# Hyena filter product on one core: second matmul over 128 partitions in place of 64

## Chip, cores and metric

The kernel runs on one core of a Trainium2 chip. The metric is the device time of one execution in microseconds. Three runs of the kernel before took 2377.81, 2381.3 and 2377.95 us, with a median of 2377.95 us.

## What is computed

The reference is a two-layer network over 256 latent and 256 context tokens of width 1024. Each layer is a half-step SwiGLU, a token mixing of two branches (gated linear attention, and an order-2 Hyena convolution), and a second half-step SwiGLU. The part that the change touches makes the Hyena filters, once for each layer, from positions alone:

```python
def hyena_filters(L, f_w1, f_b1, f_fr1, f_w2, f_b2, f_fr2, f_w3):
    ...
    h = jnp.sin(f_fr1 * (z @ f_w1 + f_b1))
    h = jnp.sin(f_fr2 * (h @ f_w2 + f_b2))
    h = (h @ f_w3).astype(jnp.float32).reshape(L, 2, HY_ORDER, HY_WIDTH)
    ...
    return h * window[:, None, None, :]
```

Here L is 256, the hidden width 64, and `f_w3` has 4096 columns (2 directions, 2 orders, 1024 channels). The product `h @ f_w3` is the one in question.

## The kernel before, in words

Activations lie with features on the partitions and 512 tokens (context, then latent) along the free axis. Weights come as chunks of eight 128x128 tiles (512 KB). Each chunk is loaded by SP, cast on ScalarE to a high part `whi` (L221), and VectorE subtracts to get the low part `wlo` (L222); up to three split chunks are kept. Every product of the layers is then three matmuls of the fp32r type (`mm3`, L382 to L384): high times high, high weight times low activation, low weight times high activation. In the stages `ffn1h` (gate and up) and `ffn1d` (down) of layer 0 and of layer 1, where both streams are worked on, those matmuls have 512 columns.

Beside these projections a second kind of work is laid into the program by `Fill`: generators that advance some steps after each projection (`fill.slot()`), in two lanes, at a pace set by deadlines counted in projections. Two of them run beside `ffn1`: `ada_gen` (modulation vectors, on VectorE at L639, fed by its own loads `adat`) and `filter_gen`, which makes the Hyena filters. The order of all instructions on an engine is thus fixed when the program is built.

`filter_gen` first makes the hidden activation `h2` (L879 to L882). Its weights `fw2` are stored twice side by side, so rows 64 to 127 of `h2` repeat rows 0 to 63. `h2s[:, 0]` is the high part and `h2s[:, 1]` the low part, each 128 rows by 256 positions. The third weights are stored twice one above the other; `split_w3` (L899) leaves their high part in rows 0 to 63 of `w3` and their low part in rows 64 to 127. Then, for each of 4 channel quarters and 2 orders, one step multiplies them. It takes two banks of PSUM (tile names ending in `_x_fil`), and for two halves of the positions (`par`) and two directions (`d`) it issues a pair of matmuls: the first (L922) has all 128 rows, high part of `h2` against high and low weights at once; the second (L923) has the low part of `h2` against the high weights and uses rows 0 to 63 alone. The position half of `h2s` is the stationary operand (128 columns), and `w3` streams 256 columns past it. So a step is eight matmuls, and there are eight steps in each layer, 16 in the program. VectorE then multiplies both banks by a window (L925, L926), and later steps normalise the filters (L939 to L954) and transform them with `mm3` on the tiles `_x_fdft` (L956 to L960).

Of the kernel before, what the change touches and what calls it, by code (L numbers as in the profile page):

```python
# [46 lines left out]
HY_HIDDEN = 64  # L47
# [27 lines left out]
def first_units():  # L75
    """The first hidden tiles of the whole program, in the order of their rows."""
    out = []
    for k in range(KT):
        for j in range(FIRST):
            out += mat("ffn1_w_gate", 0, j * P, [k])  # L80
            out += mat("ffn1_w_up", 0, j * P, [k])
    return out
# [119 lines left out]
class WS:  # L202
    """The stream of weight tiles: loaded in the order of use, split into a high and a low part."""
# [21 lines left out]
    def need(self, tiles):  # L225
        """Loads what the next tiles take."""
        for i in range((self.pos + tiles - 1) // CHUNK + 1):
            self._load(i)

    def ahead(self, tiles, i):  # L230
        """Loads the i-th chunk of those that start the given number of tiles from here, out of turn and into a pool that
        has room."""
        pos = self.pos + tiles
        while pos < len(self.plan) and self.plan[pos] is None:
            pos += 1
        self._load(pos // CHUNK + i, True)
# [40 lines left out]
class Fill:  # L277
    """Work that runs in the shadow of the projections, a few steps after each of them, at the pace that its deadline
    (counted in projections) asks for. In every step the tensor engine's part comes first and rests only on earlier
    steps."""  # L280
# [40 lines left out]
def build(tc, a, dbg=None):  # L321
    nc = tc.nc
    with ExitStack() as ctx:
# [27 lines left out]
        def opnd(w, p=actp, tag="act", name="op"):  # L351
            """High and low part of a matmul operand, w columns each."""
            if w == T:
                t = pair(p=p, tag=tag, name=name)
                return t[:, 0], t[:, 1]
            if spare.get(name):
                return spare.pop(name)
            t = pair(p=p, tag=tag, name=name)
            spare[name] = (t[:, 1, :L], t[:, 1, L:])
            return t[:, 0, :L], t[:, 0, L:]  # L360

        def plain(n, w, name):
            """n fp32 tiles of w columns."""
            out = []
            while len(out) < n:
                t = pair(F32, name=name).rearrange("p a b -> p (a b)")
                out += [t[:, i * w:(i + 1) * w] for i in range(2 * T // w)]
            return out
# [10 lines left out]
        mm = nc.tensor.matmul  # L379
# [48 lines left out]
        def quad_sum(srcs, kind, between=lambda: None):  # L428
            """Sums over the partitions of each tile: row 32 j + any of the result holds tiles j, j + 4, ... added up."""
            n = srcs[0].shape[-1]  # L430
            st = bank(kind)
            rounds = len(srcs) // 4
            for r in range(rounds):
                if r:
                    between()
                for j in range(4):
                    mm(st[32 * j:32 * j + 32, :n], lhsT=ones[:, :32], rhs=srcs[r * 4 + j], start=r == 0, stop=r == rounds - 1)
            ss = t2((P, n), name="ss")
            nc.scalar.copy(ss, st[:, :n])
            return ss  # L440

        def inv_sqrt(out, src):
            """(src) ** -0.5 for a few columns in SBUF."""
            nc.gpsimd.tensor_tensor(out=out, in0=src, in1=half[:, :src.shape[-1]], op=ALU.pow)

        def rstd(ms):
            """1 / rms of tokens, from their mean squares and epsilon."""
            nt = ms.shape[-1]
            r = sm.tile([P, nt], F32, tag="rs", name=nm("rs"))
            inv_sqrt(r, ms)  # L450
            return r

        def spread(r):
            """The same along the free axis of all partitions."""
            pr = bank("nbc")
            for i in range(r.shape[-1]):
                mm(pr[:, i * P:(i + 1) * P], lhsT=r[:, i:i + 1].broadcast_to([P, P]), rhs=ident, start=True, stop=True)
            return pr[:, :r.shape[-1] * P]
# [6 lines left out]
        class Squares:  # L465
            """Mean squares of the tokens, as the feature tiles are done: all but the last two for both streams at once."""
# [48 lines left out]
        def norm_gen(l, m, s, h, sums):  # L515
            """The norm of one stream, in steps between which the tensor engine does other things."""
            sh, sca = mods[(l, m)], mods[(l, m + 1)]
            vv = 1 - s
            r = rstd(sums.total(s))
            yield  # L520
            r = spread(r)
            if sums.early is not None:
                sums.early.r = t2((P, L), name="r")
                nc.scalar.copy(sums.early.r, r)
            for k in range(KT):
                modulate(k, s, r, sca[:, vv, k:k + 1], sh[:, vv, k:k + 1], h)
                if k % 2:
                    yield

        class Early:  # L530
            """Products of the latent tokens before their norm is known: with x * scale, and with the shift in a column of its
            own. The norm's factor comes in afterwards."""
# [32 lines left out]
        class Beside:  # L565
            """Runs the steps of a generator at given counts of calls."""
# [14 lines left out]
        def v_part(o, wv, h, tt, k):  # L581
            """Values of a tile of tokens, token-major."""
            xh, xl = h[k][0][:, tt * P:(tt + 1) * P], h[k][1][:, tt * P:(tt + 1) * P]
            mm(o, lhsT=xh, rhs=wv[k][0], start=k == 0, stop=False)
            mm(o, lhsT=xh, rhs=wv[k][1], start=False, stop=False)
            mm(o, lhsT=xl, rhs=wv[k][0], start=False, stop=k == KT - 1)

        def first_split(jobs, h, pend, v=None):
            """The first products after a norm, stream by stream: jobs are (result by stream, weights). Besides, values of
            the first stream's tokens."""  # L590
# [18 lines left out]
        def mod_finish(l, m, raw, nv):  # L609
            """raw[:, v, j]: j-th feature tile of modulation m for vector v (0 latent, 1 context)."""  # L610
# [11 lines left out]
        def ada_gen(ms):  # L622
            # silu(c) along the free axis
# [27 lines left out]
        def start():  # L651
            """First norm and first hidden tiles, a feature tile at a time as its modulation arrives. The tensor engine's
            clock is kept up while it waits for the first data."""
# [132 lines left out]
        def out_tiles(take, src, gate, streams, after):  # L786
            """The products of src that go into x, and the next norm unless x is not done yet."""
# [32 lines left out]
        def tail(take, src, gate, sums, after):  # L820
            """The last two output tiles, one stream after the other, so that the next norm of the first runs beside
            the second. Returns the norm of the second, to be run."""
# [43 lines left out]
        def filter_gen(l):  # L866
# [32 lines left out]
            def split_w3(wb):  # L899
                """High part above, low part below."""  # L900
# [12 lines left out]
            for q in range(NQ):  # L913
                for o in range(2):
# [3 lines left out]
                    for par in range(2):  # L918
                        cp = slice(par * P, (par + 1) * P)
                        for d in range(2):  # L920
                            f = pf[d][:, par * CQ:(par + 1) * CQ]
                            mm(f, lhsT=h2s[:, 0, cp], rhs=w3[:, d], start=True, stop=False)  # L922
                            mm(f, lhsT=h2s[:HY_HIDDEN, 1, cp], rhs=w3[:HY_HIDDEN, d], start=False, stop=True)  # L923
# [61 lines left out]
        def la_gen(l, asp, wap, bs):  # L985
            """Cumulative log decays (times 16) within the chunks, for every head and direction."""
# [94 lines left out]
        def gla_core(l, hd, bs, kT, qT, vp, rp, og):  # L1081
# [23 lines left out]
            def attend(d):  # L1105
                """Masked scores within tiles of two chunks. From the tile's first chunk (in the order of the scan) to its
                second, keys decay to the end of the one and queries from the start of the other."""
# [10 lines left out]
            def widen(d):  # L1118
                """From chunks to tiles: keys decay to the end of the tile, queries from its start."""
# [17 lines left out]
            def update(d):  # L1137
                """The state at the start of every tile."""
# [72 lines left out]
        def short_conv(l, j, ps, c, both):  # L1211
            """c[:, t] = w0 u[t-1] + w1 u[t] + w2 u[t+1] + b along rows (context: one row, latent: grid rows)."""
# [15 lines left out]
        def hy_proj(l, q, h):  # L1228
            """Returns z (time-major, [t, stream, channel] for the even and for the odd time steps, split), x1 (likewise, as
            it is) and x2 (channel-major)."""  # L1230
# [129 lines left out]
        def hy_conv_lat(l, q, z, x1, x2, z3):  # L1360
            """The same for the latent tokens alone: real and imaginary parts, or even and odd time steps, side by side."""
# [211 lines left out]
def fold(x):  # L1573
    """(rows, cols) with rows = k * 128 + p  ->  (128, k * cols)"""
    r, c = x.shape
    return x.reshape(r // P, P, c).transpose(1, 0, 2).reshape(P, (r // P) * c)
# [88 lines left out]
```

## Time and profile before

| what | value |
|---|---|
| median of 3 runs | 2377.95 us |
| runs | 2377.81, 2377.95, 2381.3 us |
| span of the profiled execution, first to last instruction | 2375.0 us |
| median run less that span | 2.95 us |
| TensorE busy, of the span | 2358.3 us |
| VectorE busy | 1666.0 us |
| ScalarE busy | 946.9 us |
| mean granted TensorE clock | 0.998 |

The profiled execution has no time of its own beside its span, so the span is set against the median run. PE is TensorE's matmuls, PEld its weight loads, DVE VectorE, ACT ScalarE, POOL GpSimd. A matmul's duration in the trace reaches into that of the next, because they are pipelined; what a stream of them costs is read from start to start. Its entry names the rows used of the array, as in 64\*128, and the operand that streams, as in 64x256.

### The profile page before, as it was taken

The page shows a single profiled execution, that of the slowest core. Times are in us where ns is not written, and L with a number is a line of the kernel's source. Part 1 is how long each engine was busy: PE and PEld are TensorE (multiplying, and loading weights), DVE is VectorE, ACT ScalarE, POOL GpSimd, SP SyncE. Part 2 cuts the span into 40 slices and gives each one's busy share as a digit, 9 for nine tenths or more (in the row PEclk, how much of TensorE's full clock was granted, in tenths as well). Part 3 has the DMA queues.
Part 4 walks back from the last instruction along what each step waited for, and adds up shares of the span by engine and source line. Part 5 has one row for each costly group of instructions (what it writes and reads, how often), then busy time and mean ns, then how long its engine had stood idle before and what let it go on. Part 6 is the DMA issues. An engine that isn't in the chain of part 4 may idle for free.

```text
span 2375.0 us, 33612 instructions
## 1 busy us (share of the span) xinstructions
PE 2358.3 (99%) x13300; PEld 2039.0 (86%) x13300; DVE 1666.0 (70%) x2613; ACT 946.9 (40%) x1422; POOL 114.4 (5%) x102
## 2 busy tenths in 40 slices
PE   9999999999999999999999999999999999999998
PEld 6788888888888888898888898888888999999998
DVE  4876775666779989677577756656566888868554
ACT  4432333544433334432222333323334555646444
POOL 0000011000000000010000010000011000001001
PEclk9999999999999999999999999999999999999999
DMA  7544444232243333436556535445343233555553
GB/s 273 188 146 148 156 152 151 92 107 98 98 133 124 124 116 101 140 109 201 177 169 205 176 119 166 148 146 163 125 140 116 73 128 126 168 180 173 185 186 125
DMA packets 108126, 347.52 MB, mean 146 GB/s; under 512 B 12014, under 2 KB 19008, under 8 KB 107968
## 3 DMA queue, kind: packets, MB, share of 16 engines
q1 hardware_dynamic: 107968, 345.37, 44.4%
q8 instruction: 104, 1.70, 0.3%
q14 instruction: 54, 0.44, 0.1%
HBM read 332.74 MB, written 12.58 MB: 145 GB/s over the span
## 4 chain that ended last, share of the span: by engine, by line
PE 92%; DVE 4%; issue 1%; ACT 1%; DMA 1%; POOL 1%; POOLq 0%; DVEq 0%; SPq 0%; ACTq 0%
PE L1ffn1h_acc_main L382 3%; PE L1ffn1h_acc_main L383 3%; PE L0ffn2h_acc_main L382 3%; PE L1ffn1h_acc_main L384 3%; PE L0ffn2h_acc_main L383 3%; PE L0ffn2h_acc_main L384 3%; PE L0ffn1h_acc_main L382 3%; PE L0ffn1h_acc_main L384 3%; PE L0ffn1h_acc_main L383 3%; PE L0hy_acc_main L384 2%; PE L0hy_acc_main L382 2%; PE L0hy_acc_main L383 2%; PE L1ffn2h_acc_main L382 2%; PE L1ffn2h_acc_main L383 2%; PE L1ffn2h_acc_main L384 2%; PE L0ffn1d_acc_main L382 2%
## 5 line engine op out<-in xcount | busy, mean ns | idle before, releaser
L221 ACT CAST whi<-raw 128x1024 fp32r<-128x1024 f32 x440 | 460.7, 1049 | 844.1 <-issue 311.4
L222 DVE TENSOR_TENSOR wlo<-raw,whi 128x1024 fp32r<-128x1024 f32 x440 | 538.2, 1225 | 213.3 <-ACT whi L221 210.9
L639 DVE SCALAR_TENSOR_TENSOR trash<-adat,sc 128x1024 bf16<-128x1024 f32 x224 | 275.8, 1231 | 170.6 <-DMA adat<-in_adaT 166.9
L382 PE MATMUL L1ffn1h_acc_main<-h,whi 128*128 128x512 f32 (+1 forms) x376 | 144.2, 384 | 0.0
L384 PE MATMUL L1ffn1h_acc_main<-h,wlo 128*128 128x512 f32 (+1 forms) x376 | 142.1, 378 | 0.0
L383 PE MATMUL L1ffn1h_acc_main<-h,whi 128*128 128x512 f32 (+1 forms) x376 | 142.0, 378 | 0.0
L384 PE MATMUL L0ffn2h_acc_main<-h,wlo 128*128 128x512 f32 (+1 forms) x376 | 141.2, 376 | 0.0
L383 PE MATMUL L0ffn2h_acc_main<-h,whi 128*128 128x512 f32 (+1 forms) x376 | 141.2, 376 | 0.0
L382 PE MATMUL L0ffn2h_acc_main<-h,whi 128*128 128x512 f32 (+1 forms) x376 | 141.0, 376 | 0.0
L382 PE MATMUL L0ffn1h_acc_main<-h,whi 128*128 128x512 f32 x304 | 120.4, 396 | 0.0
L384 PE MATMUL L0ffn1h_acc_main<-h,wlo 128*128 128x512 f32 x304 | 118.5, 390 | 0.0
L383 PE MATMUL L0ffn1h_acc_main<-h,whi 128*128 128x512 f32 x304 | 118.4, 390 | 0.0
L383 PE MATMUL L1ffn2h_acc_main<-h,whi 128*128 128x256 f32 x328 | 92.8, 283 | 0.0
L384 PE MATMUL L1ffn2h_acc_main<-h,wlo 128*128 128x256 f32 x328 | 92.8, 283 | 0.0
L382 PE MATMUL L1ffn2h_acc_main<-h,whi 128*128 128x256 f32 x328 | 92.7, 283 | 0.0
L375 ACT CAST g<-sg 128x512 fp32r<-128x512 f32 (+1 forms) x88 | 49.6, 566 | 107.7 <-DVE sg L775 107.7
L479 POOL TENSOR_TENSOR sq<-sq,sq 128x512 f32<-128x512 f32 (+1 forms) x30 | 40.3, 1343 | 1070.5 <-ACT sq L473 1042.6
L382 PEld LDWEIGHTS L1ffn1h_acc_main<-h,whi 128*128 128x128 f32 x376 | 71.5, 190 | 13.9 <-issue 0.7
L384 PEld LDWEIGHTS L1ffn1h_acc_main<-h,wlo 128*128 128x128 f32 x376 | 71.4, 190 | 13.1
L383 PEld LDWEIGHTS L1ffn1h_acc_main<-h,whi 128*128 128x128 f32 x376 | 71.5, 190 | 12.4
L384 PEld LDWEIGHTS L0ffn2h_acc_main<-h,wlo 128*128 128x128 f32 x376 | 70.8, 188 | 12.9
L383 PEld LDWEIGHTS L0ffn2h_acc_main<-h,whi 128*128 128x128 f32 x376 | 70.8, 188 | 12.8 <-DVE h L510 0.2
(721 smaller groups left out, 6516.5 us busy)
## 6 DMA issues: line engine op xcount, KB each, us to landing
raw<-in_w SPq DMA_DIRECT2D x440, 512.0 KB, 3.6
adat<-in_adaT SPq DMA_DIRECT2D x128, 512.0 KB, 4.0
adaw<-in_ada SPq DMA_DIRECT2D x16, 512.0 KB, 9.7
hscr<-H SPq DMA_DIRECT2D x32, 256.0 KB, 4.4
H<-hscr SPq DMA_DIRECT2D x32, 256.0 KB, 4.1
sc<-in_cb SPq DMA_DIRECT2D x8, 512.0 KB, 5.2
w3b<-in_fw SPq DMA_DIRECT2D x16, 256.0 KB, 3.8
x<-in_xT SPq DMA_DIRECT2D x8, 256.0 KB, 5.7
```

Source lines behind the costliest of these rows:

```text
L221: nc.scalar.copy(hi, raw)
L222: nc.vector.tensor_tensor(out=lo, in0=raw, in1=hi.bitcast(F32), op=ALU.subtract)
L375: nc.scalar.copy(hi, src)
L382: mm(out, lhsT=w[0], rhs=xh, start=first, stop=False)
L383: mm(out, lhsT=w[0], rhs=xl, start=False, stop=False)
L384: mm(out, lhsT=w[1], rhs=xh, start=False, stop=last)
L479: nc.gpsimd.tensor_tensor(out=t, in0=self.sum, in1=t, op=ALU.add)
L639: nc.vector.scalar_tensor_tensor(out=trash, in0=wt, scalar=1.0, in1=sc[vv], op0=ALU.mult, op1=ALU.mult, accum_out=raw[:, vv, j:j + 1])
```

## The change

One line of `filter_gen` is altered: the second matmul of each pair takes all 128 rows of the low part of `h2` and of `w3`, in place of rows 0 to 63. Its result gains the product of the low part of `h2` with the low part of the weights. The other differences between the two files are comments and docstrings that are emptied, with the line numbers kept.

```diff
                             mm(f, lhsT=h2s[:, 0, cp], rhs=w3[:, d], start=True, stop=False)
-                            mm(f, lhsT=h2s[:HY_HIDDEN, 1, cp], rhs=w3[:HY_HIDDEN, d], start=False, stop=True)
+                            mm(f, lhsT=h2s[:, 1, cp], rhs=w3[:, d], start=False, stop=True)
```

The number and the order of the instructions are the same on every engine.

## Rows read from the trace of the kernel before

**Rows 1.** The page: the span, and TensorE's busy time, share and instructions.

```profile
span 2375.0 us, 33612 instructions
...
PE 2358.3 (99%) x13300; PEld 2039.0 (86%) x13300; DVE 1666.0 (70%) x2613; ACT 946.9 (40%) x1422; POOL 114.4 (5%) x102
```

**Rows 2.** The page: the chain of work that ended last, shares by engine.

```profile
PE 92%; DVE 4%; issue 1%; ACT 1%; DMA 1%; POOL 1%; POOLq 0%; DVEq 0%; SPq 0%; ACTq 0%
```

**Rows 3.** Waits of PE, whole program: waiter, releaser, us in total, times, longest.

```profile
PE start_x_idle L658 <- DVE zeros L418: 1.5, 1, 1.5
...
PE L1ffn1h_x_nbc L457 <- POOL rs L444: 1.0, 1, 1.0
...
PE L1hy_x_du L1147 <- DVE S L1150: 0.2, 1, 0.2
```

**Rows 4.** Stretches: length, busy PE PEld DVE ACT POOL, clock, DMA share, GB/s.

```profile
97.00:168.00 71.00, 71.00 (x319) 57.83 (x318) 53.52 (x76) 26.76 (x38) 4.75 (x4) 1.00 0.45 149
1450.00:1520.00 70.00, 70.00 (x310) 56.87 (x309) 45.67 (x60) 25.32 (x36) 4.84 (x4) 1.00 0.45 146
```

**Rows 5.** Lines L922, L923: ns min/median/max; idle before; who waited (us, times).

```profile
L922 PEld LDWEIGHTS L0ffn1h_x_fil<-w,h2s x24: 186/186/188, 97.7 to 365.0; 128*128 128x128 f32 x24
L922 PE MATMUL L0ffn1h_x_fil<-w,h2s x24: 276/383/385, 97.9 to 365.0; 128*128 128x256 f32 x24
L923 PEld LDWEIGHTS L0ffn1h_x_fil<-w,h2s x24: 182/183/183, 98.1 to 365.3; 64*128 64x128 f32 x24
...
  issue: 3.8, 16
...
  DVE hf L925: 24.9, 15
```

**Rows 6.** Timeline of PE at the first step: start, duration (us), instruction.

```profile
97.66 0.39 PE L384 MATMUL L0ffn1h_acc_main<-h,wlo 128*128 128x512 f32 x1
97.89 0.28 PE L922 MATMUL L0ffn1h_x_fil<-w,h2s 128*128 128x256 f32 x1
98.09 0.38 PE L923 MATMUL L0ffn1h_x_fil<-w,h2s 64*128 64x256 f32 x1
98.41 0.38 PE L922 MATMUL L0ffn1h_x_fil<-w,h2s 128*128 128x256 f32 x1
...
100.28 0.50 PE L382 MATMUL L0ffn1h_acc_main<-h,whi 128*128 128x512 f32 x1
100.61 0.39 PE L383 MATMUL L0ffn1h_acc_main<-h,whi 128*128 128x512 f32 x1
```

**Rows 7.** Timeline of PEld (weight loads) at the same step.

```profile
97.67 0.19 PEld L922 LDWEIGHTS L0ffn1h_x_fil<-w,h2s 128*128 128x128 f32 x1
98.09 0.18 PEld L923 LDWEIGHTS L0ffn1h_x_fil<-w,h2s 64*128 64x128 f32 x1 [0.24 <-issue]
```

**Rows 8.** Timeline of PE at the transform (`fdft`) of that step's filters, twelve matmuls.

```profile
122.67 0.28 PE L382 MATMUL L0ffn1h_x_fdft<-hsh,dfth 128*128 128x256 f32 x1
...
123.99 0.28 PE L384 MATMUL L0ffn1h_x_fdft<-hsh,dftl 128*128 128x256 f32 x1
124.11 0.40 PE L382 MATMUL L0ffn1h_acc_main<-h,whi 128*128 128x512 f32 x1
124.34 0.40 PE L383 MATMUL L0ffn1h_acc_main<-h,whi 128*128 128x512 f32 x1
```

**Rows 9.** Timeline of PEld within that transform.

```profile
122.79 0.19 PEld L384 LDWEIGHTS L0ffn1h_x_fdft<-hsh,dftl 128*128 128x128 f32 x1
122.91 0.19 PEld L382 LDWEIGHTS L0ffn1h_x_fdft<-hsh,dfth 128*128 128x128 f32 x1
```

**Rows 10.** Waits from 97 to 380 us: ScalarE's cast of the next chunk.

```profile
ACT whi L221 <- PE L0ffn1h_acc_main L383: 36.6, 14, 4.4
```

**Rows 11.** The stretch around layer 1's first norm, columns as in rows 4.

```profile
1400.00:1425.00 25.00, 23.98 (x172) 22.68 (x171) 14.76 (x33) 7.92 (x15) 1.62 (x1) 0.93 0.17 50
```

## The prediction

> **What bounds the kernel now.** I read the page first. TensorE is busy for 2358.3 of the 2375.0 us of the span [rows 1], and the chain that ended last is TensorE's for 92% [rows 2]. A busy TensorE may still be one that is slow, so this alone doesn't say that time can be had, only where. Next come the waits: TensorE waited for another engine 17 times in the whole program, once in each of 17 places, between 1.5 and 0.2 us [rows 3]. Then the stretches in which the filter steps run, about 97 to 368 us and 1450 to 1755 us: TensorE is busy through all of two samples, VectorE for 53.52 of 71 us and 45.67 of 70 us, ScalarE for less, and the DMA engines have a share of 0.45 [rows 4]. There TensorE is the only limit, and a microsecond less of its work should be a microsecond less of the program.
>
> So what does a filter step cost TensorE? The line view [rows 5] shows the two matmuls of a pair, and the timeline [rows 6] shows how they follow each other. The last 512-column matmul ahead of a step starts 0.23 us before the step's first matmul, as in any stream of them. Then the eight matmuls of the step start 0.31 us apart, except the second, at 0.20 us. The matmul after the step takes 0.33 us to the next start in place of 0.23. From the start of the step (97.89) to the second projection matmul behind it (100.61) it is 2.72 us.
>
> Set against this the transform of the same filters, a few steps later [rows 8]. It too has matmuls of 256 columns and 128 stationary columns, three into the same piece of PSUM, but all of them with 128 rows. Its twelve start from 122.67 to 123.99, 11 intervals of 0.12 us. The projection after it has its usual 0.23 us to the next.
>
> The weight loads tell why. In the transform they start 0.12 us apart, each 0.19 us long, beneath the matmul that is running [rows 9]. In the filter step the load for L922 comes ahead of its matmul (97.67 against 97.89), but the one for L923 starts with its matmul (98.09), after 0.24 us in which the loader idled though nothing that the profile shows held it [rows 7]; that idle time is there in all 16 steps, 3.8 us in total [rows 5]. From there on loads and matmuls start together. The load is thus on TensorE's path wherever a 64-row matmul follows a 128-row one or the other way round, and that is at every boundary of the step but its first.
>
> **The change, part by part.** Nothing is added, removed or moved: each engine keeps its instructions and their order. The 64 matmuls at L923 (four in each of 16 steps), and their loads, get 128 rows.
>
> - *The matmul itself.* With 64 rows the load takes 183 ns, with 128 rows 186 ns [rows 5]. If loads stayed exposed, this would cost 64 x 3 ns = 0.2 us. Beneath a matmul it costs nothing, and the cover is the running matmul.
> - *The boundaries.* All eight matmuls of a step, and the projections on both sides, then have one shape of rows. No row shows L922 and L923 with it, so I bound the interval: 0.12 us below, as in the transform, 0.31 us above, as now. I take 0.12, since the transform is the nearest row in every respect that is left: type, rows, both column counts, accumulation into the same bank, same neighbours.
> - *Sum.* Eight intervals of 0.12 and one projection interval of 0.23 are 1.19 us, in place of 2.72. A step gains 1.53 us, and the 16 gain 24.5 us.
> - *New waits.* The matmul reads rows 64 to 127 of `w3` and of the low part of `h2`. Of `w3` the matmul just ahead of it reads the same rows already; of the low part one instruction writes all 128 rows. So nothing is waited for that was not waited for before.
> - *Who is late next.* VectorE waits for L923 in 15 steps, 24.9 us in total [rows 5]; it gets its first bank about 0.9 us sooner. TensorE will ask for weights sooner, by 1.53 us in some 37. ScalarE, which splits them first, waits for TensorE to free the buffers (14 times, 36.6 us, in the first stretch [rows 10]), so the split chunks stand ready with two chunks in hand. The 17.5 us that VectorE has free in 71 cover two steps' gain, 3.1 us.
>
> Against the span of 2375.0 us the sum gives 2350.5. The median run stands 2.95 us above that span, and I carry this over: 2377.95 - 24.5 = 2353.4 us.
>
> The clock matters for the range. Around the first norm of layer 1 the granted clock has a mean of 0.93 over 25 us [rows 11], so there was a short time at 1.2 in place of 2.4 GHz, after TensorE had waited 1.0 us for the norm's factor [rows 3]; it cost about 0.07 x 25 = 1.75 us. The mean clock of 0.998 over the span leaves 4.8 us of this kind in all, so most of the small pauses are followed by none. Everything behind the filter steps now comes 12 to 24 us earlier, so this one may vanish, and up to three others may appear, which I can't tell beforehand.
>
> **The rivals.**
>
> *The loads stay exposed.* The cause might be not the change of rows but something that stays, such as the stationary slices of `h2s`, or `w3` streaming twice in succession. Then the interval stays at 0.31 us, and the time is 2377.95 + 0.2 = 2378.1 us. For it speaks that no row shows just this pair at 128 rows; against it, that the transform streams the same operand twice in succession too, and its intervals are 0.12 us [rows 8]. Chance 0.03. The Trainium skill has a rule for this outcome: in "TensorE: Matmul & The Clock Gate", Part 3, The mechanism, a weight load is said to overlap a running matmul only when the two use different row groups. By that rule 128-row loads could never hide behind 128-row matmuls, and the change would give nothing. The trace disagrees: the loads of the transform start 0.12 us apart and last 0.19 us, with the same 128 rows as the matmuls above them [rows 8, 9].
>
> *Half of it.* The loads hide only in part, and the interval falls to 0.20 us, the one that the trace shows once in each step [rows 6]. Then a step has 8 x 0.20 + 0.33 = 1.93 us, gains 0.79, and the time is 2377.95 - 16 x 0.79 = 2365.3 us. Nothing in the transform speaks for it. Chance 0.04.
>
> *The weight split becomes the bound.* VectorE gets its two window products earlier, in the midst of other work, and the next `wlo` comes late. Then TensorE waits at a projection and the gain is given back, at most to 2378 us. Against it stand VectorE's free time and the chunks in hand. Chance 0.02.
>
> *Slower, by the clock.* The pauses of TensorE [rows 3] are 17. Were each followed by a time at 1.2 GHz like that of rows 11, for 1.75 us each, this would cost 29.8 us, and the time would be 2377.95 - 24.5 + 29.8 = 2383.2 us. It decides from 14 such places on (14 x 1.75 = 24.5). Before, the mean clock of 0.998 leaves room for not even three of them in the whole span, so 14 is far off. Chance 0.01.
>
> **How the numbers follow.** The forecast has a chance of 0.90. Its own range: the clock can give back 1.75 us, and a start-to-start read to 0.01 us leaves some 16 x 0.08 = 1.3 us each way, so 2350.5 below. Above, three more such places (5.25 us) and the rounding give 2360.0. The other cases together hold 0.10 and lie outside, so the range can stop there. A measurement of this kernel can tell about 0.2%, or 4.8 us, from no change. Faster by more than that are the forecast and the half case, 0.94; within it lie the exposed loads and the late split, 0.05; slower is the clock's, 0.01.
>
> **What would show it.** In the profile of the changed kernel L923 should read 128\*128, its matmuls last about 283 ns as in the transform, and the starts in a step stand 0.12 us apart, with the projection behind it at 0.40 in place of 0.50 us. The loader's 3.8 us of idle time ahead of L923 should be gone, and VectorE's wait for L923 fall by some 14 us of its 24.9. TensorE should still be busy throughout both stretches, and the span be near 2350.5 us. Intervals of 0.2 or 0.3 us would prove the reading of the boundaries wrong; intervals of 0.12 with a span above 2360 us would prove that the gain was lost elsewhere, and the waits of TensorE or the granted clock would show where.

## The result and the profile after

The changed kernel takes 2353.45 us (median of four runs, 2351.53 to 2355.46), the kernel before 2377.98 us beside it (four runs, 2377.81 to 2381.3). The ratio is 0.9898 with a 95% interval of 0.9886 to 0.991: 24.5 us less. On two other chips the changed kernel took 2352.88 us (ratio 0.989, 0.9873 to 0.9906) and 2352.89 us (0.9894, 0.9878 to 0.9911).

| what | before | after |
|---|---|---|
| median | 2377.98 us | 2353.45 us |
| profiled span | 2375.0 us | 2349.7 us |
| that execution's own time | | 2351.53 us |
| TensorE busy | 2358.3 us | 2332.4 us |
| mean granted clock | 0.998 | 0.998 |

The busy times on the page of the kernel after, as in [rows 1]:

```profile
PE 2332.4 (99%) x13300; PEld 2030.9 (86%) x13300; DVE 1667.0 (71%) x2613; ACT 947.0 (40%) x1422; POOL 112.5 (5%) x102
```

TensorE has the same 13300 matmuls and is 25.9 us less busy, though 64 of them now use twice the rows. The profiled execution is the fastest of the four runs; the median is the figure to compare. The timeline of TensorE at the first filter step of the kernel after (start and duration in us) answers to [rows 6]:

```profile
97.58 0.39 PE L384 MATMUL L0ffn1h_acc_main<-h,wlo 128*128 128x512 f32 x1
97.80 0.28 PE L922 MATMUL L0ffn1h_x_fil<-w,h2s 128*128 128x256 f32 x1
97.92 0.28 PE L923 MATMUL L0ffn1h_x_fil<-w,h2s 128*128 128x256 f32 x1
98.04 0.28 PE L922 MATMUL L0ffn1h_x_fil<-w,h2s 128*128 128x256 f32 x1
...
98.76 0.40 PE L382 MATMUL L0ffn1h_acc_main<-h,whi 128*128 128x512 f32 x1
98.99 0.40 PE L383 MATMUL L0ffn1h_acc_main<-h,whi 128*128 128x512 f32 x1
```

Every interval within the step is 0.12 us, and the projection behind it has 0.23 to the next start. From 97.80 to 98.99 it is 1.19 us, where it was 2.72 us. The weight loads of the same step, as in [rows 7], show why:

```profile
97.58 0.19 PEld L922 LDWEIGHTS L0ffn1h_x_fil<-w,h2s 128*128 128x128 f32 x1
97.81 0.19 PEld L923 LDWEIGHTS L0ffn1h_x_fil<-w,h2s 128*128 128x128 f32 x1
97.92 0.19 PEld L922 LDWEIGHTS L0ffn1h_x_fil<-w,h2s 128*128 128x128 f32 x1
```

The load for L923 starts at 97.81, with the matmul ahead of its own, and lies beneath it. Before, it started together with its own matmul.

Line L923 of the kernel after (ns min/median/max; who waited, us and times) answers to [rows 5]:

```profile
L923 PEld LDWEIGHTS L0ffn1h_x_fil<-w,h2s x24: 187/192/192, 97.8 to 352.9; 128*128 128x128 f32 x24
L923 PE MATMUL L0ffn1h_x_fil<-w,h2s x24: 282/283/283, 97.9 to 353.0; 128*128 128x256 f32 x24
...
  DVE hf L925: 14.2, 8
```

A load has become longer by 9 ns in its median (192 against 183) and costs nothing, since it is hidden. The loader's idle time ahead of it, 3.8 us in 16 steps, is gone.

Where the time went can be read from the start of the two mixing stages, which follow the filter steps of either layer. The rows of line L382 on their banks give the first start, for the kernel before,

```profile
L382 PE MATMUL L0mixA_acc_main<-h,whi x48: 279/283/363, 430.2 to 449.5; 128*128 128x256 f32 x48
L382 PE MATMUL L1mixA_acc_main<-h,whi x32: 283/283/386, 1803.9 to 1824.8; 128*128 128x256 f32 x32
```

and for the kernel after:

```profile
L382 PE MATMUL L0mixA_acc_main<-h,whi x48: 278/283/366, 417.6 to 437.0; 128*128 128x256 f32 x48
L382 PE MATMUL L1mixA_acc_main<-h,whi x32: 279/283/386, 1777.9 to 1798.7; 128*128 128x256 f32 x32
```

Layer 0's filter steps brought 12.6 us (8 x 1.53 = 12.2; 0.1 us of the lead stood already ahead of the first step), and by layer 1's mixing the lead is 26.0 us, 1.5 us more than the 24.5 of all 16 steps. Two things in between account for 1.05 of these 1.5 us, one of them a gain of 1.75 and the other a loss of 0.7; the rest was not traced. Around layer 1's first norm the granted clock, which had a mean of 0.93 over 25 us [rows 11], stayed at 1.00 in the same stretch of this execution (0.07 x 25 = 1.75 us):

```profile
1388.00:1413.00 25.00, 23.98 (x178) 22.41 (x177) 16.22 (x35) 8.72 (x18) 1.62 (x1) 1.00 0.19 67
```

And TensorE has one wait of note that it did not have, of 0.7 us for a weight chunk at the end of layer 0 (waits of PE, kernel after):

```profile
PE L0ffn2d_acc_main L384 <- DVE wlo L222: 0.7, 1, 0.7
```

Neither is a fixed property of the kernel. In a second profiled execution of the changed kernel, on another chip, that wait was 0.2 us, and the stretch from 1825 to 1850 us, in layer 1's mixing, had a mean clock of 0.93, where the execution shown here has 1.00.

### The profile page after: what moved, and what is told of

It reads as the page before. It is cut to its first block, busy times and chain, and to the rows that moved or that the text cites. A ratio compares the mean times of both kernels' runs of the same rounds, so it can differ in the third digit from the quotient of the medians.

```text
span 2349.7 us, 33612 instructions
## 1 busy us (share of the span) xinstructions
PE 2332.4 (99%) x13300; PEld 2030.9 (86%) x13300; DVE 1667.0 (71%) x2613; ACT 947.0 (40%) x1422; POOL 112.5 (5%) x102
## 4 chain that ended last, share of the span: by engine, by line
PE 91%; DVE 4%; issue 1%; ACT 1%; DMA 1%; POOL 1%; POOLq 0%; DVEq 0%; SPq 0%; ACTq 0%
PE L1ffn1h_acc_main L382 3%; PE L0ffn2h_acc_main L382 3%; PE L0ffn2h_acc_main L383 3%; PE L1ffn1h_acc_main L383 3%; PE L0ffn2h_acc_main L384 3%; PE L1ffn1h_acc_main L384 3%; PE L0ffn1h_acc_main L382 3%; PE L0ffn1h_acc_main L383 3%; PE L0ffn1h_acc_main L384 3%; PE L0hy_acc_main L384 2%; PE L0hy_acc_main L383 2%; PE L0hy_acc_main L382 2%; PE L1ffn2h_acc_main L382 2%; PE L1ffn2h_acc_main L384 2%; PE L1ffn2h_acc_main L383 2%; PE L1ffn1d_acc_main L383 2%
## 5 line engine op out<-in xcount | busy, mean ns | idle before, releaser
L221 ACT CAST whi<-raw 128x1024 fp32r<-128x1024 f32 x440 | 460.7, 1049 | 850.2 <-issue 329.9
L382 PE MATMUL L1ffn1h_acc_main<-h,whi 128*128 128x512 f32 (+1 forms) x376 | 142.8, 380 | 0.0
L382 PE MATMUL L0ffn2h_acc_main<-h,whi 128*128 128x512 f32 (+1 forms) x376 | 141.0, 376 | 0.0
L382 PE MATMUL L0ffn1h_acc_main<-h,whi 128*128 128x512 f32 x304 | 119.8, 394 | 0.0
L382 PE MATMUL L1ffn2h_acc_main<-h,whi 128*128 128x256 f32 x328 | 92.7, 283 | 0.0
L382 PEld LDWEIGHTS L1ffn1h_acc_main<-h,whi 128*128 128x128 f32 x376 | 70.8, 188 | 13.2 <-issue 0.7
L383 PEld LDWEIGHTS L0ffn2h_acc_main<-h,whi 128*128 128x128 f32 x376 | 70.8, 188 | 12.8 <-DVE h L510 0.2
L382 PEld LDWEIGHTS L0ffn2h_acc_main<-h,whi 128*128 128x128 f32 x376 | 70.6, 188 | 12.9
```

The lines of the kernel that those rows point to most:

```text
L221: nc.scalar.copy(hi, raw)
L382: mm(out, lhsT=w[0], rhs=xh, start=first, stop=False)
L383: mm(out, lhsT=w[0], rhs=xl, start=False, stop=False)
```

## The experiments

In all of them the length of a step is read as in the prediction: from the start of the last projection matmul ahead of it to the start of the second one behind it, less the 0.23 us that belong to the first of these. The kernel before has 2.72 us, the changed one 1.19. A boundary is a place where the number of rows changes from one matmul to the next. A load is exposed where it starts with its own matmul, and hidden where it starts earlier, beneath the matmul ahead. The medians of the kernel before differ by 1.6 us from chip to chip (2376.81 to 2378.4), so a variant is set against runs on its own chip where there are any.

**Fewer boundaries, same work.** The 64-row matmuls of the kernel before stay, but the order is 128, 128, 64, 64.

```diff
                         for d in range(2):
-                            f = pf[d][:, par * CQ:(par + 1) * CQ]
-                            mm(f, lhsT=h2s[:, 0, cp], rhs=w3[:, d], start=True, stop=False)
-                            mm(f, lhsT=h2s[:HY_HIDDEN, 1, cp], rhs=w3[:HY_HIDDEN, d], start=False, stop=True)
+                            mm(fs[d], lhsT=h2s[:, 0, cp], rhs=w3[:, d], start=True, stop=False)
+                        for d in range(2):
+                            mm(fs[d], lhsT=h2s[:HY_HIDDEN, 1, cp], rhs=w3[:HY_HIDDEN, d], start=False, stop=True)
```

> The kernel before, with the order within each half of the positions changed: both 128-row matmuls first, then both 64-row ones. A step then has four boundaries between 128 and 64 rows in place of eight; work, rows and operands are the same. Before and changed kernel differ by 2.72 - 1.19 = 1.53 us in a step over eight boundaries, 0.19 us for each. Theory (a load is exposed only where the row count changes from one matmul to the next): four exposed loads, a step of 1.19 + 4 x 0.19 = 1.95 us, 16 x 0.77 = 12.3 us gained, about 2365.7 us, and intervals of about 0.12 to 0.22 us in a step, none of 0.31. Rival (a 64-row matmul exposes its own load and the load behind it, whatever its neighbour): six exposed loads, 2.33 us in a step, 6.2 us gained, about 2371.8 us. Rival (only the count of rows worked on matters): no change, 2378 us.

Measured: 2366.41 us (2365.44 to 2371.14) against 2376.81 for the kernel before on that chip, ratio 0.996 (0.9945 to 0.9974). The timeline of its first step, in which the view shows each like pair as one row (x2):

```profile
98.02 0.39 PE L384 MATMUL L0ffn1h_acc_main<-h,wlo 128*128 128x512 f32 x1
98.25 0.43 PE L922 MATMUL L0ffn1h_x_fil<-w,h2s 128*128 128x256 f32 x2
98.61 0.50 PE L924 MATMUL L0ffn1h_x_fil<-w,h2s 64*128 64x256 f32 x2
99.04 0.50 PE L922 MATMUL L0ffn1h_x_fil<-w,h2s 128*128 128x256 f32 x2
99.47 0.50 PE L924 MATMUL L0ffn1h_x_fil<-w,h2s 64*128 64x256 f32 x2
99.90 0.50 PE L382 MATMUL L0ffn1h_acc_main<-h,whi 128*128 128x512 f32 x1
100.24 0.40 PE L383 MATMUL L0ffn1h_acc_main<-h,whi 128*128 128x512 f32 x1
```

The step takes 100.24 - 98.02 - 0.23 = 1.99 us, near the 1.95 of four boundaries and far from the 2.33 of six. It is the odd one, since the loader waited 0.19 us there for `w`; the other 15 steps take 1.95 us each. So a 64-row matmul can hide its load, behind another with 64 rows. The median is 10.4 us below that of the kernel before and not 12.3, while the two fastest runs lie 11.4 us below it. The profiled execution is the slowest of the four (2371.14 us), and it shows a loss outside the steps. At the end of layer 0 TensorE waited 3.09 us for a chunk, whose cast stood on ScalarE behind a work item that waits for its own load, and the 25 us from 1375 us on had a mean clock of 0.86:

```profile
1382.12 1.06 ACT L628 ACTIVATE sc<-sc 128x1024 f32<-128x1024 f32 x1 [5.20 <-DMA sc<-in_cb]
1383.08 1.03 ACT L221 CAST whi<-raw 128x1024 fp32r<-128x1024 f32 x1
...
1384.16 0.55 PE L382 MATMUL L0ffn2d_acc_main<-g,whi 128*128 128x256 f32 x1 [3.09 <-ACT whi L221]
```

**All eight with 64 rows.** Half of the first matmul's rows are left out.

```diff
-                            mm(f, lhsT=h2s[:, 0, cp], rhs=w3[:, d], start=True, stop=False)
+                            mm(f, lhsT=h2s[:HY_HIDDEN, 0, cp], rhs=w3[:HY_HIDDEN, d], start=True, stop=False)
                             mm(f, lhsT=h2s[:HY_HIDDEN, 1, cp], rhs=w3[:HY_HIDDEN, d], start=False, stop=True)
```

> The kernel before with 64 rows for the first matmul too, so that all eight of a step have 64 rows; it leaves out the high part of h2 times the low part of the weights. Theory (only a change of the row count exposes a load): two exposed loads, into the step and out of it; a step of 1.19 + 2 x 0.19 = 1.57 us, 18.4 us gained, about 2359.6 us, intervals within the step 0.12 us. Rival (a 64-row matmul exposes its load whatever its neighbour): nine exposed loads, 2.90 us in a step, 2.9 us lost, about 2381 us.

Measured: 2358.18 us (2357.31 to 2359.23), ratio 0.9921 (0.9906 to 0.9936), 18.6 us less than before. The timeline of its first step:

```profile
98.07 0.39 PE L384 MATMUL L0ffn1h_acc_main<-h,wlo 128*128 128x512 f32 x1
98.39 0.38 PE L922 MATMUL L0ffn1h_x_fil<-w,h2s 64*128 64x256 f32 x1
98.61 0.28 PE L923 MATMUL L0ffn1h_x_fil<-w,h2s 64*128 64x256 f32 x1
98.73 0.28 PE L922 MATMUL L0ffn1h_x_fil<-w,h2s 64*128 64x256 f32 x1
...
99.53 0.50 PE L382 MATMUL L0ffn1h_acc_main<-h,whi 128*128 128x512 f32 x1
99.86 0.39 PE L383 MATMUL L0ffn1h_acc_main<-h,whi 128*128 128x512 f32 x1
```

The step takes 1.56 us (expected 1.57). The two matmuls at the boundaries, L922 at 98.39 and L382 at 99.53, are the long ones (0.38 and 0.50 us); between them 64-row matmuls follow each other at 0.12 us, just as 128-row ones do. It is the change of rows that costs, not their number. Using half the rows for the same count of matmuls is thus slower than using all of them: by 6.1 us against the variant with 96 rows below, which ran on the same chip, and two exposed loads in each of 16 steps are 16 x 2 x 0.19 = 6.1 us.

**96 and 72 rows.** Two variants, with the second matmul's rows cut to a part of the array. The diff is that of 96 rows, against the changed kernel.

```diff
-                            mm(f, lhsT=h2s[:, 1, cp], rhs=w3[:, d], start=False, stop=True)
+                            mm(f, lhsT=h2s[:96, 1, cp], rhs=w3[:96, d], start=False, stop=True)
```

> The second matmul takes 96 rows in place of 64 or 128; of the low part of h2 times the low part of the weights it thus adds half. Theory in its plain form (any change of the row count exposes the load): eight boundaries as before, a step of 2.72 us, about 2378 us. Rival (what counts is a class of array size, and 96 rows fall into that of 128): no exposed load, intervals of 0.12 us, about 2353.5 us.

> The second matmul takes 72 rows; of the low part of h2 times the low part of the weights it adds an eighth. After the run with 96 rows: if every count above 64 belongs to the class of 128, no load is exposed, a step takes 1.19 us, and the time is about 2353 us. Rival (96 was a case of its own, as three quarters of the array): eight exposed loads, 2.72 us in a step, about 2378 us.

Measured: 2352.13 us (2350.96 to 2353.25; ratio 0.9894, 0.9877 to 0.991) with 96 rows (four runs), and 2353.54 us with 72 (a single run). The timeline with 96 rows:

```profile
98.47 0.28 PE L922 MATMUL L0ffn1h_x_fil<-w,h2s 128*128 128x256 f32 x1
98.58 0.29 PE L923 MATMUL L0ffn1h_x_fil<-w,h2s 96*128 96x256 f32 x1
98.70 0.29 PE L922 MATMUL L0ffn1h_x_fil<-w,h2s 128*128 128x256 f32 x1
98.83 0.28 PE L923 MATMUL L0ffn1h_x_fil<-w,h2s 96*128 96x256 f32 x1
```

Here the plain form of the theory fell. A change from 128 to 96 rows, or to 72, exposes nothing; the intervals are 0.11 to 0.13 us, in the trace with 72 rows as in this one. What counts is a class of row numbers, that is a set of row counts between which a change costs nothing. The two counts tried above 64 are in the class of 128.

**64 and 32 rows in turn.**

```diff
-                            mm(f, lhsT=h2s[:, 0, cp], rhs=w3[:, d], start=True, stop=False)
-                            mm(f, lhsT=h2s[:HY_HIDDEN, 1, cp], rhs=w3[:HY_HIDDEN, d], start=False, stop=True)
+                            mm(f, lhsT=h2s[:HY_HIDDEN, 0, cp], rhs=w3[:HY_HIDDEN, d], start=True, stop=False)
+                            mm(f, lhsT=h2s[:32, 1, cp], rhs=w3[:32, d], start=False, stop=True)
```

> The first matmul of a pair takes 64 rows, the second 32; left out are the high part of h2 times the low part of the weights, and half of the low part of h2 times the high part of the weights. If 32 and 64 rows are classes of their own, each of the eight matmuls and the projection behind them meets a boundary: nine exposed loads, 1.19 + 9 x 0.19 = 2.90 us in a step, about 2381 us. Rival (only the full class sets itself apart, and all counts up to 64 are one class): two exposed loads as with 64 rows throughout, 1.57 us in a step, about 2359 us.

Measured: 2391.82 us in a single run, against 2377.91 for the kernel before on that chip, where its seven runs go from 2376.23 to 2386.63. The timeline of its second step (its first is lengthened by the clock, as told below):

```profile
136.97 0.39 PE L384 MATMUL L0ffn1h_acc_main<-h,wlo 128*128 128x512 f32 x1
137.29 0.38 PE L922 MATMUL L0ffn1h_x_fil<-w,h2s 64*128 64x256 f32 x1
...
139.77 0.50 PE L382 MATMUL L0ffn1h_acc_main<-h,whi 128*128 128x512 f32 x1
140.10 0.40 PE L383 MATMUL L0ffn1h_acc_main<-h,whi 128*128 128x512 f32 x1
```

The step takes 140.10 - 136.97 - 0.23 = 2.90 us, the value of nine exposed loads: 32 and 64 rows are two classes (no count between them was tried). Nine boundaries instead of eight account for 16 x 0.18 = 2.9 us of the 13.9 us by which it is slower. Most of the rest is the clock, told of below.

**TensorE as the limit, from the other side.** The first matmul of a pair is issued twice in the changed kernel.

```diff
+                            mm(f, lhsT=h2s[:, 0, cp], rhs=w3[:, d], start=True, stop=True)
                             mm(f, lhsT=h2s[:, 0, cp], rhs=w3[:, d], start=True, stop=False)
                             mm(f, lhsT=h2s[:, 1, cp], rhs=w3[:, d], start=False, stop=True)
```

> The changed kernel with each first matmul of a pair issued twice, the second of the two starting its sum anew: 64 more matmuls of 128 rows and 256 columns, and nothing else. If TensorE is the only limit in these stretches, each costs its interval of 0.12 us: 64 x 0.12 = 7.7 us more than the changed kernel, about 2361.1 us. Rival (another engine has become the limit after the change, and TensorE has time to spare there): less than half of that, about 2353.5 to 2357 us.

Measured: 2363.85 us, with a wide scatter (2359.3 to 2369.38); ratio 0.9946 (0.993 to 0.9962). In its first step the twelve matmuls run from 98.14 to the second projection at 99.80, 1.66 us, so four more cost 0.47 us, as expected. The same holds over whole stretches. From the first projection of layer 0's `ffn1h` to the first of its mixing stage the changed kernel takes 354.1 us and the variant 358.0, and in layer 1 it is 390.4 and 394.1. That makes 3.9 and 3.7 us for 32 additional matmuls each (32 x 0.12 = 3.8), so TensorE has no time to spare there. The time itself is 10.4 us over the changed kernel's 2353.45, more than 7.7. In the profiled execution the surplus lies at the place at the end of layer 0 that the first experiment showed: a wait of 2.3 us for a chunk (L382 for ScalarE's cast, L221), and a mean clock of 0.93 over the 25 us around it, where the changed kernel had 1.00.

**A change of type.** The trace shows a long projection matmul behind one more thing: the plain fp32 matmul that sums each filter's columns (L939). The variant makes that sum an fp32r matmul, to see whether a change of type costs what a change of rows does.

```diff
-                    nc.gpsimd.tensor_tensor(out=af[:, :CQ], in0=af[:, :CQ], in1=af[:, CQ:], op=ALU.add)
+                    afr = t2((P, CQ), F32R, name="afr")
+                    nc.gpsimd.tensor_tensor(out=afr, in0=af[:, :CQ], in1=af[:, CQ:], op=ALU.add)
...
-                    mm(po[:, :CQ], lhsT=ones, rhs=af[:, :CQ], start=True, stop=True)
+                    mm(po[:, :CQ], lhsT=ones_r, rhs=afr, start=True, stop=True)
```

> The changed kernel with the filters' column sum (L939) as an fp32r matmul, its operand rounded to that type by the addition that makes it, in place of plain fp32. In the changed kernel the two passes of that sum and the projection behind it take 0.24 + 0.43 = 0.67 us from start to start. If the change of type exposes a load as the change of rows does, the fp32r sum takes 0.12 and the projection 0.23 us: 0.32 us less in each of 16 steps, 5.1 us, about 2348.3 us. Rival (only the second pass costs, and the boundary's time stays): 0.12 us less in each, about 2351.5 us.

> The changed kernel again, unaltered, on the same chip as the column-sum variant: near 2353.5 us, so that the two can be set side by side.

Measured: 2349.67 us (2347.51 to 2353.95) against 2352.88 (2351.68 to 2353.98) for the changed kernel, with ranges that overlap. So it was repeated with the constant's copy (`ones_r`) moved from the program's start into the first filter step:

> The column sum in fp32r again, with the fp32r copy of its constant operand made in the first filter step and not at the start of the program, where the first variant began its weight products 0.4 us later. Each sum and the projection behind it take 0.35 in place of 0.67 us, 5.1 us in 16 steps: 4 to 5 us below the changed kernel on the same chip, about 2348.5 us. Rival (what the first variant showed is run-to-run scatter): within 2 us of the changed kernel.

> The changed kernel, unaltered, beside the column-sum variant on the same chip: 2352 to 2354 us.

Measured: 2348.48 us (2347.64 to 2351.84; ratio to before 0.9878, 0.9863 to 0.9893) against 2352.89 us (2352.79 to 2353.44), 4.4 us less. The runs of the two do not overlap. The sum in the changed kernel on that chip,

```profile
110.46 0.59 PE L939 MATMUL L0ffn1h_x_fst<-af,ones 128*128 128x256 f32 x2
110.70 0.59 PE L382 MATMUL L0ffn1h_acc_main<-h,whi 128*128 128x512 f32 x1
111.13 0.40 PE L383 MATMUL L0ffn1h_acc_main<-h,whi 128*128 128x512 f32 x1
```

and in the variant, where its line is L942:

```profile
110.23 0.28 PE L942 MATMUL L0ffn1h_x_fst<-afr,ones_r 128*128 128x256 f32 x1
110.35 0.39 PE L382 MATMUL L0ffn1h_acc_main<-h,whi 128*128 128x512 f32 x1
110.58 0.39 PE L383 MATMUL L0ffn1h_acc_main<-h,whi 128*128 128x512 f32 x1
```

0.67 us became 0.35, and the projection behind the sum has its usual 0.23 us to the next start in place of 0.43. This version is ahead of both kernels. Its cause is another than the one that was tried, though. Plain fp32 matmuls of the same size stand in a row elsewhere (L1181 and L1184, each matmul two rows, so x2 is one and x4 two), with no change of type between them, here in the changed kernel on that chip:

```profile
606.21 1.03 PE L1184 MATMUL L0hy_x_o<-S,qd 128*128 128x256 f32 x4
607.07 0.59 PE L1181 MATMUL L0hy_x_o<-v,att 128*128 128x256 f32 x2
607.50 1.03 PE L1184 MATMUL L0hy_x_o<-S,qd 128*128 128x256 f32 x4
608.18 0.58 PE L382 MATMUL L0hy_acc_main<-h,whi 128*128 128x512 f32 x1
608.60 0.40 PE L383 MATMUL L0hy_acc_main<-h,whi 128*128 128x512 f32 x1
```

Two of them take 0.86 us and one takes 0.43. The last two and the projection behind them take 1.10 us, which is 2 x 0.43 + 0.23 and leaves 0.01 us for the change back to fp32r. By this price a lone sum and its projection take 0.43 + 0.23 = 0.66 of the 0.67 us. So the 0.32 us saved are the price of plain fp32, 0.43 against 0.12 us, and no row shows that a change of type exposes a load; the projection only starts early in the record, within the sum's 0.43 us.

## Why the prediction was right

- *The bound.* TensorE was the only limit in the two stretches, and still is. The gain of the steps arrived whole at the next stage (12.6 us for layer 0), and additional matmuls lengthened both stretches by their own time (3.9 and 3.7 us for 3.8).
- *The term that carries the sum.* 1.53 us a step was read from two neighbouring places of one trace; it measured 1.53 us. That the time came out within 0.1 us of the forecast is luck, since the four runs lie 3.9 us apart. The choice of 0.12 us over 0.31 for the new interval was right, and so was the reason: the loads hide again. Steps with 0, 2, 4, 8 and 9 changes of class took 1.19, 1.56, 1.95 (1.99 in the first), 2.72 and 2.90 us, and 1.19 + 0.19 for every change gives 1.19, 1.57, 1.95, 2.71 and 2.90. The prediction spoke of a change of rows; the runs with 96 and 72 rows narrow this to a change of class.
- *The rule on row groups.* By the rule of the Trainium skill that the first rival named, no load would have hidden under matmuls of the same rows. The new loads of L923 do, 0.12 us apart and 0.19 us long. Another page of the Trainium skill fits the runs: "TensorEngine Tiling (Array Packing)" lists row tilings of 128, 64 and 32 rows (Tiling Modes) and says that changing the tiling mode drains the engine (Key Properties). The trace shows the price, 0.19 us, and that a load is not begun ahead across such a change. Whether the engine is empty meanwhile, no row here tells.
- *New waits.* None came from the added operand rows. One of 0.7 us came at a place that the prediction did not look at, the end of layer 0, behind both filter stretches of that layer; it is the late weight split of the third rival, but small, elsewhere, and not the same in each execution (0.2 us in another).
- *The clock.* The short time at a lower clock around layer 1's first norm did vanish in the profiled execution, and its span fell by 25.3 us, more than the 24.5 of the steps. In another execution of the same kernel one appeared in layer 1's mixing. That one may go and another come was said beforehand; which, was not. Across the runs the medians agree with the sum without any of it.
- *The 2.95 us between run and span.* They are not a fixed part. After the change the profiled execution's own time is 1.83 us above its span, so some 1.1 of the 2.95 us say only that the profiled execution before was quicker than the median. In the forecast of the time this cancels, because the gain is taken from the median.
- *The lower end of the range.* Its terms add to 2353.4 - 1.75 - 1.3 = 2350.35, not 2350.5. Nothing hangs on it.
- *Mis-sized side figures.* VectorE's wait for L923 was to fall by some 14 us of 24.9; it fell by 10.7, to 14.2 us. The load with 128 rows was to take 186 ns and took 192. Both were off the path and changed nothing.

## What to carry to other kernels

Look for matmuls with few rows between matmuls with many: if the loader's row idles ahead of them and loads start together with their matmuls, each change of class puts some 0.19 us on TensorE's path. That figure holds for the shapes tried here (fp32r, 128 stationary and 256 moving columns, projections of 512 columns beside them). Where the operands already fill the other partitions with something harmless or useful, take all the rows; otherwise put matmuls of one class next to each other. Intervals also show the price of a type: a lone plain fp32 matmul among fp32r ones cost 0.43 us here against 0.12. Price such a place from a row of its own kind before putting it down to the boundary.

## What the runs showed of the hardware that was not expected

The granted clock fell behind seven of the 16 steps that alternate 64 and 32 rows, in the single run of that variant. The stretch around the first step has a mean clock of 0.87,

```profile
95.00:103.00 8.00, 8.00 (x29) 5.75 (x28) 6.55 (x11) 2.30 (x3) 0.00 (x0) 0.87 0.58 181
```

although TensorE counts as busy for all 8 us, and the projections behind that step have 0.42 us from start to start in place of 0.23; that is the lower of the two levels, 1.2 in place of 2.4 GHz. The mean over the span was 0.993; against the 0.998 of before this is about 0.005 x 2390 = 12 us, which with the 2.9 us of boundaries covers the 13.9 us measured. Behind all the steps, at 1872 us, there is one more such time, with no step ahead of it. Steps with 64 rows throughout showed none of it (mean clock 0.999), nor did those of the kernel before. The loads were exposed in the kernel before and 64 rows alone did not lower the clock, so in the executions profiled neither did it alone; whether it takes both, or the 32 rows, was not tried apart.

Also, the end of layer 0 is a place where a few microseconds are lost or not from kernel to kernel. ScalarE's next cast can stand behind `sc` (L628), which waits for its own load; TensorE waited there 3.09 us in the grouped variant, 2.3 us with the additional matmuls, and 0.7 us, for the low part, in one execution of the changed kernel and 0.2 us in another. Taking that wait away was not tried.
